# Short-convolution input: c and u of four feature tiles as two jobs of seven block products

## Chip, core and metric

One core of one Trainium2 chip runs the whole kernel in one launch. The metric is the device time of that launch in microseconds (us), lower is better. Differences of a few us in about a thousand are at stake, so every term below is worked out in tenths of a us.

## What is computed

The reference is a two-layer decoder trunk on 512 tokens of width 1024, in float32. Only the start of the first layer is touched by the change:

```python
def short_conv_mixer(h, w_in, conv_w, w_out):
    bcx = h @ w_in                                   # 1024 -> 3 x 1024
    b_gate, c_gate, u = jnp.split(bcx, 3, axis=-1)
    y = b_gate * causal_depthwise_conv3(c_gate * u, conv_w)
    return y @ w_out

h = x
mix = short_conv_mixer(rmsnorm(h, a_pre_norm[l]), a_w_in[l], a_conv_w[l], a_w_out[l])
h = h + rmsnorm(mix, a_post_norm[l])
```

After it come a SwiGLU feed-forward, a sliding-window attention with sinks, and a second feed-forward. They are the same in both kernels.

## The kernel before

**Number format.** Every matrix product is made of three TensorE passes. A factor is split in a high part (`whi`, `xhi`: a copy rounded to fp32r, made by ScalarE) and a low part (`wlo`, `xlo`: the remainder, a subtraction on VectorE), and `mm3` (L203 to L207) adds whi*xlo, whi*xhi and wlo*xhi in PSUM. So a weight tile of 128x1024 costs one ScalarE instruction and one VectorE instruction (L490, L491) before TensorE may use it.

**The convolution stage.** Features lie on the partitions, the 512 tokens along the free dimension. The 1024 features of each of c, u and b are eight tiles, f = 0 to 7. A projection (`project`, L209) is one such tile: eight blocks of the contraction, three passes each, 24 matmuls of 512 columns into one PSUM bank. The norm of x is not applied to x: a row of factors `rows` (one per token, made by `square`, a power on GpSimd, and the matmuls `pr` at L746 and L747) is multiplied into each projection as it is taken out of PSUM (L767, L770, L783). For each feature tile VectorE then runs three tap instructions (`taps`, L774 and L777), GpSimd multiplies c by u (L771) and the taps by b (L784), and `pair_sums` (L602 to L612) makes the sums and splits that the output projection needs. That projection is itself done by seven block products for the first four feature tiles (`P1` to `P7`, function `seven`).

**What sets the order.** The stage stands in a list, `CONV`: "c2" is the projection of c for tile 2, "P1" a block product, "w0" a weight tile that is only split. Tiles 0 and 1 are written out ahead of the list. `in_line` (L495) walks the list. While job j runs on TensorE it emits the split of the weights of job j+3 (`LINE_LEAD = 3`) and the loads that the seven buffers of raw weights (`N_RAW`) allow, and then the late parts of an earlier job (taps, gates, sums), all but one of those that are due in one go. The instructions of each engine run in the order in which they are emitted, and each engine waits on semaphores. Four pairs of whi and wlo exist (`N_W = 4`). GpSimd's queue also issues DMAs that add up weight blocks in DRAM for the later stages (`sum_on`, `issue`, L559). x is loaded transposed (`xt`) for the projections and once in its own layout (`hs`) for the squares and for the residual update.

Of the kernel before, what the change touches and what calls it, by code (L numbers as in the profile page):

```python
# [16 lines left out]
P = 128  # L17
# [20 lines left out]
    "c2 u2 b2 c3 u3 b3 c4 u4 b4 c5 u5 P1 P5 b5 P6 P3 c6 P7 P2 u6 P4 b6 w0 c7 u7 w1 b7 w2 w3"  # L38
)

# [41 lines left out]
def yoco_kernel(  # L82
# [8 lines left out]
    w_in: bass.AP,  # L91
    w_ob: bass.AP,
# [134 lines left out]
    xt = [halves("xt") for _ in range(KT // 2)]  # L227
    xt = [xt[k // 2][k % 2] for k in range(KT)]
# [217 lines left out]
    class Raw:  # L446


        def __init__(self, *srcs):
            self.srcs = srcs  # L450
            self.widths = [s.shape[0] * S if len(s.shape) == 3 else D for s in srcs]
            self.n = sum(self.widths)

        def fetch(self):
            self.tile, c = wraw.tile([P, D], F32, tag="raw", name=name("raw")), 0
            for src, n in zip(self.srcs, self.widths):
# [4 lines left out]
                nc.sync.dma_start(dst, src)  # L461
                c += n

    class Job:
# [10 lines left out]
        def add(self):  # L475
            if self.make:
                raw = self.raws[0].tile
                nc.vector.tensor_tensor(out=raw, in0=raw, in1=self.raws[1].tile, op=ALU.add)  # L478
# [16 lines left out]
    def in_line(jobs, late, paced=True):  # L495
# [9 lines left out]
        def prepare(j):  # L505
# [3 lines left out]
            while n[0] < len(raws) and (n[0] < N_RAW or raws[n[0] - N_RAW].last <= j):  # L509
                raws[n[0]].fetch()  # L510
                n[0] += 1
# [156 lines left out]
    rows = slot("rrow")  # L668
# [6 lines left out]
    sums = small.tile([P, 4], F32, tag="sums", name=name("sums"))  # L675
    squares = wide("squares")

    def square(b):
        nc.scalar.activation(squares, hs[b], AF.Square, scale=1 / 32,
                             accum_out=sums[:, b : b + 1])  # L680

    with tc.manual_schedule(engines=ALL):

        warm = small.tile([P, 1], F32, tag="warm", name=name("warm"))
        nc.scalar.activation(warm, ones[:, 0:1], AF.Copy)
        idle = bank("idle", ps_pt)
        for _ in range(WARM):
            nc.tensor.matmul(idle[:, :P], ones, ones, start=True, stop=True)

        def first_hi(i, c0, c1):  # L690
            nc.scalar.activation(ws[i][0][:, c0:c1], first[i][:, c0:c1], AF.Copy)

        def first_lo(i, c0, c1):
            nc.vector.tensor_tensor(out=ws[i][1][:, c0:c1], in0=first[i][:, c0:c1],
                                    in1=ws[i][0][:, c0:c1].bitcast(F32), op=ALU.subtract)

        def token_hi(k):
            nc.scalar.activation(xs[k][0], xt[k], AF.Copy, scale=g(G_APRE, k))

        def token_lo(k):  # L700
            nc.vector.scalar_tensor_tensor(
                out=xs[k][1], in0=xt[k], scalar=g(G_APRE, k), in1=xs[k][0].bitcast(F32),
                op0=ALU.mult, op1=ALU.subtract,
            )

        FIRST = {0: [(0, 0, P), (0, P, 384)], 1: [(0, 384, 768)], 2: [(0, 768, D), (1, 0, S)],
                 4: [(1, S, D)], 5: [(2, 0, S)], 6: [(2, S, D)]}
        for k in range(KT):
            pieces = FIRST.get(k, [])
            token_hi(k)  # L710
            for p in pieces:
                first_hi(*p)
            for p in pieces:
                first_lo(*p)
            token_lo(k)
            for i in range(3):
                for t in range(3):
                    n = 3 * k + t
                    whi, wlo = (w[:, n % KT * P : (n % KT + 1) * P] for w in ws[n // KT])
                    nc.tensor.matmul(begun[0][t], (whi, wlo, whi)[i], xs[k][i == 2],  # L720
                                     start=k == i == 0, stop=k == KT - 1 and i == 2)
        later += [fetch(w_in[1, t]) for t in range(len(later), 3)]
        for b in range(NB):
            hs[b] = wide("h")
            nc.sync.dma_start(hs[b], x[b])
        nc.sync.dma_start(mask, tables[:, 2 * S :])
        nc.sync.dma_start(snk, sinks.partition_broadcast(P))
        ws = [split_weights(None, raw, True) for raw in later[:2]]
        square(0)
        square(1)  # L730
        ws.append(split_weights(None, later[2], True))
        square(2)
        square(3)
        project(begun[1][0], ws[0], xs)
        v = small.tile([P, 4], F32, tag="v", name=name("v"))
        nc.vector.tensor_scalar(out=v, in0=sums, scalar1=EPS, scalar2=None, op0=ALU.add)
        nc.gpsimd.tensor_tensor(out=cols, in0=v, in1=mhalf, op=ALU.pow)
        project(begun[1][1], ws[1], xs)
        pr = bank("pr", ps_pt)
        dg, dhi, dlo = slot("dg"), slot("dhi", F32R), slot("dlo", F32R)  # L740
        for b in range(NB):
            nc.vector.tensor_scalar(out=dg[:, b * P : (b + 1) * P], in0=ident,
                                    scalar1=cols[:, b : b + 1], scalar2=None, op0=ALU.mult)
        nc.scalar.activation(dhi, dg, AF.Copy)
        nc.vector.tensor_tensor(out=dlo, in0=dg, in1=dhi.bitcast(F32), op=ALU.subtract)
# [1001 lines left out]
```

## Time and profile before

| | us |
|---|---|
| median of 3 runs | 1013.98 (1012.76 to 1014.38) |
| profiled execution, device time | 1012.5 |
| span of its trace | 1010.7 |
| TensorE busy (PE), matmuls | 1002.3 |
| VectorE (DVE) busy | 887.7 |
| ScalarE (ACT) busy | 588.4 |
| GpSimd (POOL) busy | 203.9 |

1.8 us of the profiled execution lie outside the span of the trace. A matmul's record in the trace is longer than its place in the pipeline: a stream of them overlaps, so that the pace of a stream is read from start to start. "pcub" is a projection's PSUM bank, "raw" a weight tile as loaded, "gx", "gy", "gz" the PSUM banks of a feed-forward's block products, "wlo" and "whi" the halves of a split.

### The profile page before, as it was taken

The numbers are of one execution on the slowest core, as the hardware profiler recorded it, in microseconds if no ns is written. First come the engines' busy times: TensorE is split into PE (matmuls) and PEld (weight loads), VectorE is DVE, ScalarE is ACT, GpSimd is POOL, SyncE is SP. The second block draws the span as 40 slices with busy tenths as digits, with TensorE's granted clock in tenths as the row PEclk, the third lists the DMA queues.
The fourth block names the chain that finished last, engine by engine and source line by source line (L and its number), as shares of the span: only waits on it lengthen the run. The fifth ranks groups of instructions, "written<-read, shape, count | busy, mean of one in ns | idle before, by whom it ended". The sixth has DMA issues, their size and how long they took to land.

```text
span 1010.7 us, 16083 instructions
## 1 busy us (share of the span) xinstructions
PE 1002.3 (99%) x5864; PEld 882.4 (87%) x5864; DVE 887.7 (88%) x1525; ACT 588.4 (58%) x1061; POOL 203.9 (20%) x264
## 2 busy tenths in 40 slices
PE   9999999999999999999999999999999999999997
PEld 8888888999889898898898888789998888989986
DVE  5766767899789999999888998888997999999996
ACT  6322444875656465566385788777666564645641
POOL 0443033102101011000022657321211010110001
PEclk9999999999999999999999999999999999999999
DMA  9997789649979789779603889966999577979742
GB/s 357 293 252 241 180 248 334 185 167 268 334 246 288 250 287 311 240 214 343 209 1 120 225 236 245 303 233 176 295 288 330 167 247 235 284 277 266 247 174 84
DMA packets 66575, 244.50 MB, mean 242 GB/s; under 512 B 7872, under 2 KB 8384, under 8 KB 54720
## 3 DMA queue, kind: packets, MB, share of 16 engines
q1 hardware_dynamic: 51328, 145.98, 38.8%
q0 software_dynamic: 14592, 96.48, 37.6%
q10 hardware_dynamic: 576, 1.02, 0.3%
q8 instruction: 46, 0.75, 0.3%
q14 instruction: 33, 0.27, 0.1%
HBM read 237.15 MB, written 102.76 MB: 336 GB/s over the span
## 4 chain that ended last, share of the span: by engine, by line
PE 97%; DVE 2%; ACT 1%; issue 0%; DVEq 0%
PE gx L1093 15%; PE gx L1096 8%; PE pcub L207 4%; PE pcub L205 4%; PE pcub L206 4%; PE px L206 4%; PE px L205 4%; PE px L207 4%; PE pmix L207 3%; PE pmix L205 3%; PE pmix L206 3%; PE gz L1093 3%; PE gy L206 2%; PE gy L205 2%; PE gy L207 2%; PE pz L206 2%
## 5 line engine op out<-in xcount | busy, mean ns | idle before, releaser
L491 DVE TENSOR_TENSOR wlo<-raw,whi 128x1024 fp32r<-128x1024 f32 x225 | 274.6, 1225 | 33.8 <-ACT whi L490 33.7
L490 ACT ACTIVATE whi<-raw 128x1024 fp32r<-128x1024 f32 x225 | 233.7, 1051 | 99.1 <-DVE raw L478 28.7
L1093 PE MATMUL gx<-xt,whi 128*128 128x512 f32 x480 | 120.7, 393 | 0.0
L1093 PEld LDWEIGHTS gx<-xt,whi 128*128 128x128 f32 x480 | 86.2, 189 | 15.7
L559 POOL DMA_DIRECT2D hsum<-in_w_gb_dram x96 | 64.4, 757 | 135.0 <-ACT whi L490 89.6
L559 POOL DMA_DIRECT2D hsum<-hsum x32 | 25.3, 792 | 304.8 <-ACT whi L490 219.7
L1048 DVE TENSOR_TENSOR st<-gx,st 128x256 f32<-128x256 f32 x200 | 77.5, 419 | 2.2 <-ACT st L1071 0.4
L1071 ACT ACTIVATE st<-gx 128x256 f32<-128x256 f32 x120 | 43.5, 380 | 60.9 <-PE gx L1096 57.2
L1096 PEld LDWEIGHTS gx<-xt,wlo 128*128 128x128 f32 x480 | 65.5, 190 | 4.7
L1096 PE MATMUL gx<-xt,wlo 128*128 128x256 f32 x480 | 66.9, 282 | 0.0
L1107 ACT ACTIVATE gr<-gr 128x1024 f32<-128x1024 f32 x20 | 21.2, 1062 | 55.6 <-DVE gr L1048 55.6
L205 PE MATMUL px<-wlo,ahi 128*128 128x512 f32 x120 | 46.7, 389 | 0.0
L206 PE MATMUL px<-whi,ahi 128*128 128x512 f32 x120 | 46.7, 389 | 0.0
L207 PE MATMUL px<-whi,alo 128*128 128x512 f32 x120 | 46.7, 389 | 0.0
L205 PE MATMUL gy<-xlo,whi 128*128 128x256 f32 x160 | 45.3, 283 | 0.0
L206 PE MATMUL gy<-xhi,whi 128*128 128x256 f32 x160 | 45.3, 283 | 0.0
L207 PE MATMUL gy<-xhi,wlo 128*128 128x256 f32 x160 | 45.3, 283 | 0.0
L559 POOL DMA_DIRECT2D hsum<-in_w_dn_dram x48 | 32.6, 794 | 47.3 <-ACT whi L490 47.3
L1093 PE MATMUL gx<-xhl,whi 128*128 128x512 f32 x160 | 39.9, 391 | 0.0
L312 POOL TENSOR_TENSOR ur<-uv,mhalf 128x1 f32<-128x1 f32 x15 | 13.9, 929 | 119.8 <-DVE uv L308 119.8
L660 DVE TENSOR_TENSOR mix<-mix,px 128x512 f32<-128x512 f32 x54 | 34.8, 682 | 2.2 <-PE px L207 2.2
L478 DVE TENSOR_TENSOR raw<-raw,raw 128x1024 f32<-128x1024 f32 x28 | 34.1, 1219 | 0.0
(322 smaller groups left out, 2996.8 us busy)
## 6 DMA issues: line engine op xcount, KB each, us to landing
hsum<-in_w_gb_dram POOLq DMA_DIRECT2D x96, 512.0 KB, 8.0
raw<-hsum SPq DMA_DIRECT2D x88, 512.0 KB, 7.9
raw<-in_w_gb_dram SPq DMA_DIRECT2D x60, 512.0 KB, 7.0
hsum<-in_w_dn_dram POOLq DMA_DIRECT2D x36, 512.0 KB, 8.2
raw<-in_w_dn_dram SPq DMA_DIRECT2D x32, 512.0 KB, 6.2
hsum<-hsum POOLq DMA_DIRECT2D x28, 512.0 KB, 5.7
raw<-in_w_in_dram SPq DMA_DIRECT2D x21, 512.0 KB, 7.4
hsum<-in_w_dn_dram POOLq DMA_DIRECT2D x12, 768.0 KB, 12.1
```

Source lines behind the costliest of these rows:

```text
L205: nc.tensor.matmul(out, whi, xlo, start=start, stop=False, **kw)
L206: nc.tensor.matmul(out, whi, xhi, start=False, stop=False, **kw)
L207: nc.tensor.matmul(out, wlo, xhi, start=False, stop=stop, **kw)
L478: nc.vector.tensor_tensor(out=raw, in0=raw, in1=self.raws[1].tile, op=ALU.add)
L490: self.begun = nc.scalar.activation(hi[:, :n], raw, AF.Copy)
L491: nc.vector.tensor_tensor(out=lo[:, :n], in0=raw, in1=hi[:, :n].bitcast(F32), op=ALU.subtract)
L559: nc.gpsimd.dma_start(dst, src, max_dma_last_dim=4 * 4 * S, **kw))
L660: nc.vector.tensor_tensor(out=m, in0=m, in1=banks[bs][r], op=ALU.subtract if half else ALU.add)
L1048: nc.vector.tensor_tensor(out=out, in0=a, in1=b, op=ALU.add)
L1071: nc.scalar.activation(ste, a, AF.Copy)
L1093: nc.tensor.matmul(banks[c][e], whi[:, kk], factors[p][k][2], start=opened and k == 0, stop=False, **kw)
L1096: nc.tensor.matmul(banks[c][e][:, :256], wlo[:, kk], factors[p][k][0], start=False, stop=k == 3 and p in (4, 5), **kw)
```

## The change

Tiles 0, 1, 6 and 7 keep their projections. For tiles 2 to 5 the order is new: the four projections of b come first (`b2 b3 b4 b5`, `gate_job`), and the eight projections of c and u become two jobs, X for tiles 2 and 3 and Y for tiles 4 and 5, of seven block products each (`cross_jobs`). c and u of a pair of tiles are a two-by-two block product of weights and tokens (the contraction in two halves, the tokens in two halves of 256), and each of the seven products has 24 matmuls of 256 columns. The sums of weight blocks are made on VectorE, four of 128x1024 for each job. The sums of token blocks are made ahead, in the buffers of `xt` (`combine`, `sum_hi`, `sum_lo`), which loses the plain x; x in its own layout is loaded once for the squares, which also overwrite it (`own`), and a second time behind job Y for the residual. The product c*u comes out of PSUM in one step (the last two rows of `take`), so the factor of the norm is squared (`rows2`) and multiplied in once for both. The two matmuls `pr` stand behind the projection b1 rather than ahead of it.

```diff
-    "c2 u2 b2 c3 u3 b3 c4 u4 b4 c5 u5 P1 P5 b5 P6 P3 c6 P7 P2 u6 P4 b6 w0 c7 u7 w1 b7 w2 w3"
+    "b2 b3 b4 b5 X1 X2 X6 X5 X7 X3 X4 Y1 Y2 Y6 Y5 Y7 Y3 Y4 P1 P5 c6 P6 P3 u6 P7 P2 b6 P4 w0 c7 u7 w1 b7 w2 w3"
+CROSS = (2, 6)
...
+    def combine(k):
+        q11, q21, q12, q22 = (quarter(i, hf, k) for hf in range(2) for i in range(2))
+        g0, g1 = g(G_APRE, k), g(G_APRE, k + 4)
+        for out, a, sc, op, b in ((q11, q11, g0, ALU.subtract, q12),
+                                  (q12, q22, g1, ALU.subtract, q12),
+                                  (q22, q22, g1, ALU.add, q11),
+                                  (q21, q21, g1, ALU.subtract, q22)):
+            nc.vector.scalar_tensor_tensor(out=out, in0=a, scalar=sc, in1=b, op0=ALU.mult,
+                                           op1=op)
...
+        def square_rows():
+            nc.vector.tensor_tensor(out=cu, in0=cu, in1=rows2, op=ALU.mult)
...
+    def gate_job(f, pool):
+        def products(job):
+            ps = bank("pcub", pool)
+            project(ps, job.w, xs)
+            brs[f] = slot("bry")
+            nc.vector.tensor_tensor(out=brs[f], in0=ps, in1=rows, op=ALU.mult)
+        return Job([Raw(w_in[f, 2])], products)
+
+    def cross_jobs(f, c):
+        a11, a12, a21, a22 = (Raw(w_cu[f // 2 - 1, b]) for b in range(4))
+        both_of = Raw()
...
+        def plus(out, a, b):
+            nc.vector.tensor_tensor(out=out.tile, in0=a.tile, in1=b.tile, op=ALU.add)
+        def make_two():
+            plus(both_of, a21, a22)
+        def make_three():
+            plus(a21, a21, a11)
+            plus(a11, a11, both_of)
+        def make_four():
+            plus(a12, a12, a11)
+        raws = {1: [a11], 2: [a12, both_of, a21, a22], 6: [a11, a21, both_of], 5: [both_of],
+                7: [a21], 3: [a12, a11], 4: [a22]}
+        make = {2: make_two, 6: make_three, 3: make_four}
...
+        def take(p):
+            x, y, z = (banks.get(c) for c in "XYZ")
+            st, u, gr = kept
+            g0, g1 = (gr.rearrange("p (e h c) -> p e h c", e=2, h=2)[:, :, h] for h in range(2))
+            if p in (1, 6):
+                nc.scalar.activation(st, x, AF.Copy)
+            elif p == 5:
+                nc.scalar.activation(u, z, AF.Copy)
+            elif p == 2:
+                nc.vector.tensor_tensor(out=g0, in0=tiles(y), in1=tiles(st), op=ALU.add)
+            elif p == 3:
+                nc.vector.tensor_tensor(out=g1, in0=tiles(z), in1=tiles(st), op=ALU.add)
+            elif p == 7:
+                nc.vector.tensor_tensor(out=u, in0=x, in1=u, op=ALU.add)
+            else:
+                for gg, m in ((g0, x), (g1, u)):
+                    nc.vector.scalar_tensor_tensor(out=gg, in0=tiles(m), scalar=-1.0, in1=gg,
+                                                   op0=ALU.mult, op1=ALU.mult)
...
+                for e in range(2):
+                    for k in range(4):
+                        kk = slice(e * S + k * P, e * S + (k + 1) * P)
+                        mm3(banks[c][:, e * 256 : (e + 1) * 256], whi[:, kk], wlo[:, kk],
+                            *factors[p][k], ...)
+                take(p)
...
+        def end():
+            steps = [conv(f + e, kept[2], brs.pop(f + e)) for e in range(2)]
+            parts = [lambda: [s[0]() for s in steps], steps[0][1], steps[1][1],
+                     lambda: [s[2](None) for s in steps]]
+            for s in steps:
+                parts += s[3]()
+            return parts
...
     def late():
         parts = []
+        pr = bank("pr", ps_pt)
+        nc.tensor.matmul(pr, ones_r, dlo, start=True, stop=False)
+        nc.tensor.matmul(pr, ones_r, dhi, start=False, stop=True)
+        nc.scalar.activation(rows, pr, AF.Copy)
+        nc.scalar.activation(rows2, pr, AF.Square)
```

What follows of this in each engine's order is shown at three places. On TensorE, behind the projection b1 (its last matmul has wlo_397 before), the projections c2, u2, b2 and so on followed:

```order
L205 MATMUL pcub_245<-xlo_231,whi_395 128x512
L206 MATMUL pcub_245<-xhi_230,whi_395 128x512
L207 MATMUL pcub_245<-xhi_230,wlo_397 128x512
L205 MATMUL pcub_559<-xhl_220,whi_513 128x512
L206 MATMUL pcub_559<-xhl_220,whi_513 128x512
L207 MATMUL pcub_559<-xhl_220,wlo_514 128x512
```

Now b2 to b5 stand there, and behind b5 (pcub_734) comes the product X1, whose matmuls have half the columns:

```order
L209 MATMUL pcub_734<-xhi_230,whi_635 128x512
L210 MATMUL pcub_734<-xhi_230,wlo_636 128x512
L208 MATMUL gx_768<-xhl_220,whi_688 128x256
L209 MATMUL gx_768<-xhl_220,whi_688 128x256
L210 MATMUL gx_768<-xhl_220,wlo_689 128x256
L208 MATMUL gx_768<-xhl_221,whi_688 128x256
```

In all 192 matmuls of 512 columns are gone and 336 of 256 columns have come.

On VectorE, before, the late parts of tiles 2 and 3 (b's gate, then the pair sums of L602 to L612) stand between the low halves of two weight tiles like this; the taps stand further ahead, between other weight tiles:

```order
L783 TENSOR_TENSOR bry_691<-pcub_759,rrow_232 128x512
L602 TENSOR_TENSOR a_218_798<-yy_558,a_218_798 128x256
L605 TENSOR_TENSOR s_796<-yy_558 128x256
L606 SCALAR_TENSOR_TENSOR s_796<-s_796,yy_558 128x256
L605 TENSOR_TENSOR s_797<-yy_558 128x256
L606 SCALAR_TENSOR_TENSOR s_797<-s_796,yy_558 128x256
L612 TENSOR_TENSOR alo_842<-s_796,ahi_841 128x512
L767 TENSOR_TENSOR cru_799<-pcub_802,rrow_232 128x512
L491 TENSOR_TENSOR wlo_872<-raw_588,whi_871 128x1024
```

Now the late parts of both tiles stand in one piece between the low half of Y5's weights (wlo_1030) and that of Y7's (wlo_1086, the last row here). Ahead of these twelve rows stand wlo_1030, the two multiplications by rows2 (`gr`) and the first two taps of tile 2:

```order
L847 SCALAR_TENSOR_TENSOR t_994<-gr_767,gt,t_994 128x510
L844 TENSOR_SCALAR t_996<-gr_767,gt 128x512
L847 SCALAR_TENSOR_TENSOR t_996<-gr_767,gt,t_996 128x511
L847 SCALAR_TENSOR_TENSOR t_996<-gr_767,gt,t_996 128x510
L609 TENSOR_TENSOR a_244_999<-yy_995,a_244_999 128x256
L612 TENSOR_TENSOR s_997<-yy_995 128x256
L613 SCALAR_TENSOR_TENSOR s_997<-s_997,yy_995 128x256
L612 TENSOR_TENSOR s_998<-yy_995 128x256
L613 SCALAR_TENSOR_TENSOR s_998<-s_997,yy_995 128x256
L619 TENSOR_TENSOR alo_1050<-s_997,ahi_1049 128x512
L923 TENSOR_TENSOR gr_1002<-gy_1059,st_1000 128x2x256
L498 TENSOR_TENSOR wlo_1086<-raw_862,whi_1085 128x1024
```

On ScalarE the high half of Y7's weights (whi_1085) stands behind two conversions of the same late parts: `a_244` waits for a GpSimd product (yy_995), `ahi_1049` for a VectorE sum (s_997):

```order
L497 ACTIVATE whi_1029<-raw_861 128x1024
L608 ACTIVATE a_244_999<-yy_995 128x256
L618 ACTIVATE ahi_1049<-s_997 128x512
L497 ACTIVATE whi_1085<-raw_862 128x1024
L618 ACTIVATE ahi_1090<-s_998 128x512
L618 ACTIVATE ahi_1094<-yy_995 128x512
L919 ACTIVATE st_1000<-gx_1003 128x512
L497 ACTIVATE whi_1123<-raw_639 128x1024
```

Before, the same conversions of tiles 2 and 3 stood between whi_827 and whi_912, each about one projection apart.

More of the change, by code (lines that the diff above doesn't have):

```diff
@@ L667, in yoco_kernel @@
           for k in range(KT)]
-    rows = slot("rrow")
+    rows, rows2 = slot("rrow"), slot("rrow")
     cols = small.tile([P, 4], F32, tag="cols", name=name("cols"))
@@ L673, in yoco_kernel @@
              for f in range(2)]
[L675 to L676 removed]
+    sums = small.tile([P, 8], F32, tag="sums", name=name("sums"))
+    own = [[slot("own") for _ in range(2)] for _ in range(NB)]
     def square(b):
[L679 to L745, printed above, removed]
[L746 to L749 removed]
```

244 lines of the change are left out of this document (200 added, 44 removed).

## The prediction

> **What bounds the kernel now.** I read the page's busy times first, then the chain of work that ended last, then the waits of TensorE, and last the windows of the convolution stage.
>
> ```profile
> span 1010.7 us, 16083 instructions
> PE 1002.3 (99%) x5864; PEld 882.4 (87%) x5864; DVE 887.7 (88%) x1525; ACT 588.4 (58%) x1061; POOL 203.9 (20%) x264
> PE 97%; DVE 2%; ACT 1%; issue 0%; DVEq 0%
> PE idle L688 <- DVE ones L149: 1.1, 1, 1.1
> PE pt L1412 <- DVE plo L1429: 0.4, 1, 0.4
> 40.00:50.00 10.00, 10.00 (x46) 8.29 (x45) 7.91 (x14) 2.03 (x4) 5.57 (x7) 1.00 1.04 297
> 90.00:100.00 10.00, 10.00 (x46) 8.29 (x45) 4.68 (x6) 1.58 (x2) 2.01 (x2) 1.00 1.01 340
> ```
>
> TensorE is the chain (97%) and waits 1.5 us in the whole run. In the stage of the change it is busy 10.00 of 10 us (second number of the windows), at a granted clock of 1.00, while VectorE (fourth number) has 2 to 5 us free in ten. So matmul work saved comes off the end one for one, and a wait that TensorE did not have goes on the end one for one. Nothing behind the stage can take it back.
>
> **Part 1, the matmuls.** A projection's 24 matmuls run from the first row to the second; a product's 24 of 256 columns, in the feed-forward, from the third to the fourth.
>
> ```profile
> 149.93 0.39 PE L205 MATMUL pcub<-xhl,whi 128*128 128x512 f32 x1
> 155.37 0.39 PE L205 MATMUL pmix<-wlo,yhi 128*128 128x512 f32 x1
> 206.46 0.28 PE L205 MATMUL gy<-xlo,whi 128*128 128x256 f32 x1
> 209.34 0.63 PE L1093 MATMUL gx<-xt,whi 128*128 128x512 f32 x2
> ```
>
> That is 5.44 us a projection and 2.88 us a product: a matmul of half the columns costs 0.120 us, not half of 0.227. Eight projections go (43.5 us), fourteen products come (40.3 us). The gain is **3.2 us**, if TensorE never waits.
>
> **Part 2, what VectorE must do in the meantime.** Eight projections needed eight weight splits in 43.5 us; fourteen products need fourteen in 40.3 us, plus eight sums of 128x1024. The lead is still three jobs, now 8.6 us instead of 16.3. Prices are starts of neighbouring rows:
>
> ```profile
> 33.13 0.60 ACT L748 ACTIVATE rrow<-pr 128x512 f32<-128x512 f32 x1 [2.35 <-PE pr L747]
> 33.76 0.69 DVE L767 TENSOR_TENSOR cru<-pcub,rrow 128x512 f32<-128x512 f32 x1 [1.64 <-ACT rrow L748]
> 34.37 0.68 DVE L770 TENSOR_TENSOR cru<-pcub,rrow 128x512 f32<-128x512 f32 x1
> 41.94 0.48 DVE L774 TENSOR_SCALAR cut<-cut,gt 128x512 f32<-128x512 f32 x1
> 42.45 1.54 DVE L777 SCALAR_TENSOR_TENSOR cut<-cut,gt 128x511 f32<-128x511 f32 x2
> 43.91 0.69 DVE L783 TENSOR_TENSOR bry<-pcub,rrow 128x512 f32<-128x512 f32 x1
> 47.48 0.41 DVE L605 TENSOR_TENSOR s<-yy 128x256 f32<-128x256 f32 x1
> 49.06 0.69 DVE L612 TENSOR_TENSOR alo<-s,ahi 128x512 fp32r<-128x512 f32 x1
> 73.86 0.41 DVE L602 TENSOR_TENSOR a<-yy,a 128x256 fp32r<-128x256 f32 x1
> 57.59 1.22 DVE L491 TENSOR_TENSOR wlo<-raw,whi 128x1024 fp32r<-128x1024 f32 x1
> 58.72 0.68 DVE L783 TENSOR_TENSOR bry<-pcub,rrow 128x512 f32<-128x512 f32 x1
> 95.07 1.22 DVE L478 TENSOR_TENSOR raw<-raw,raw 128x1024 f32<-128x1024 f32 x1
> 96.20 0.69 DVE L789 TENSOR_TENSOR ylo<-bry,yhi 128x512 fp32r<-128x512 f32 x1
> ```
>
> An operation on 512 columns takes 0.60 us (33.76 to 34.37), three taps 1.97 (41.94 to 43.91), the four pair sums 1.58 (47.48 to 49.06) and the subtraction ahead of them 0.41, a split or a sum of 1024 columns 1.13.
>
> I follow VectorE to the place shown in the change, the low half of Y7's weights (wlo_1086). It can begin its first work of the stage, the taking out of tile 0, only when `rows` is there. That was at 33.76, right behind `pr`; `pr` now stands behind one more projection, so 33.76 + 5.44 = **39.2**. From there to wlo_1086 its queue holds, counted in its order:
>
> - 26 operations on 512 columns (tiles 0 and 1, the token sums of the second half, the four gates, what is taken out of X and of Y2, the two products by rows2, four low halves of pair sums): 15.6 us
> - 13 weight splits and 7 weight sums of 1024: 22.6 us
> - taps of four tiles: 7.9 us; pair sums of two pairs with their subtractions: 4.0 us
>
> That is **50.1 us** with nothing in its way. Two things are. First, GpSimd:
>
> ```profile
> 66.64 1.29 POOL L771 TENSOR_TENSOR cut<-cru 128x512 f32<-128x512 f32 x1 [5.79 <-DVE cru L770]
> 66.67 2.34 DVE L491 TENSOR_TENSOR wlo<-raw,whi 128x1024 fp32r<-128x1024 f32 x1 [0.17 <-ACT whi L490]
> 74.02 1.40 POOL L784 TENSOR_TENSOR yy<-cut,bry 128x512 f32<-128x512 f32 x1 [4.34 <-DVE bry L783]
> 75.45 0.43 DVE L605 TENSOR_TENSOR s<-yy 128x256 f32<-128x256 f32 x1 [1.18 <-POOL yy L784]
> 54.75 1.06 ACT L490 ACTIVATE whi<-raw 128x1024 fp32r<-128x1024 f32 x1 [2.78 <-issue]
> ```
>
> A split beside a GpSimd product takes 2.34 instead of 1.22 us. Three such products of the first two pairs fall beside VectorE's taps or splits (the second c*u, the first gate of each pair): **3.3 us**. Second, waits in VectorE's own queue: the second gate product of a pair starts only behind the last tap, and the pair sums stand behind it (1.18 us in the row; two pairs, 2.0), and a weight that has just been summed must go through ScalarE (1.06 us) before its low half: X3's weights fully, X6's for half of it, and two more behind ScalarE's taking out of X1 and X5, together **2.8 us**. In all 39.2 + 50.1 + 3.3 + 4.8 = 97.4: wlo_1086 is there at about 97.4.
>
> TensorE's side: `pr` began at 32.63 in the row below, so b2 begins 5.44 + 0.46 later, at 38.5; four projections and eleven products (X1 to X4, Y1, Y2, Y6, Y5) are 21.8 + 31.7 us, and two matmuls of Y7 need only its high half: it wants wlo_1086 at **92.2**.
>
> ```profile
> 32.63 0.23 PE pr L746
> ```
>
> So TensorE has waited 5.2 us by then, a little of it ahead of X6 and most at Y7, where the late parts of tiles 2 and 3 stand between two weight splits: some 11 us of VectorE's time, with its wait and its contention, against the 8.6 us of lead. Here the ScalarE order is as bad: whi_1085 stands behind a conversion that waits for the same GpSimd product.
>
> Behind it two smaller waits. Y3's weights are summed, and split behind two low halves, after wlo_1086: 1.13 + 0.60 + 0.60 + 1.13 = 3.5 us against the 2.9 us of Y7: **0.6 us**. P3's weights stand behind the taps of tiles 4 and 5: from Y4's end VectorE has one split in hand and takes out Y4 (1.9), two splits, a sum and ScalarE's part of it (4.5), the products by rows2 and the first taps (3.2); then GpSimd (1.3), three ScalarE operations on 512 columns (1.8, at the 0.60 of the row of `rows`), the high half and the low half (2.2): 14.9 us, while TensorE has P1, P5, c6, P6 (three of 2.72 us and 5.44), 13.6: **1.3 us**.
>
> The sum of the waits is 5.2 + 0.6 + 1.3 = **7.1 us**, against 3.2 gained: **3.9 us slower**.
>
> **Part 3, costed at nothing.** The sixteen token combinations and eight low halves of token sums on VectorE, with their ScalarE operations: the combinations and four of the low halves lie beside c1 and u1, where the 20 to 30 us window has VectorE busy 4.31 of 10 us; the other four are in the count above. Uncovered, the first part would be 6.3 + 2.4 us (16 at the 0.395 of a pair sum, four at 0.60), but `pr` has 5.4 us more time than before. The second loading of x (2 MB) and the halved loads of the first: the queue's loads land in 7.4 us in the median and are wanted some 70 us later. Y's last weight tiles are loaded only when X5's and X7's splits have freed buffers (about 68 and 70 us by the same counting), some 7 us ahead of their sum; late, this costs up to 4 us. GpSimd loses four products and its DMA issues come earlier; both cost TensorE nothing as long as the sums are done before the feed-forward.
>
> ```profile
> 20.00:30.00 10.00, 10.00 (x46) 8.28 (x45) 4.31 (x9) 7.71 (x13) 1.03 (x1) 1.00 1.03 405
> raw<-in_w_in_dram SPq DMA_DIRECT2D x21, 512.0 KB, 7.4
> ```
>
> **Bounds.** No row shows products of this kind fed by VectorE at this lead, so both ends stay. With no contention and no waits VectorE is done at 89.3, ahead of the 92.2, and only the 3.2 us are left. For more than I count speaks a tap instruction beside GpSimd's DMA issues, 1.51 us instead of 0.48:
>
> ```profile
> 36.36 2.23 POOL L559 DMA_DIRECT2D hsum<-in_w_gb_dram  x4
> 37.43 1.51 DVE L774 TENSOR_SCALAR cut<-cut,gt 128x512 f32<-128x512 f32 x1
> ```
>
> With three such groups of issues in its way (3.0 us) and 1.5 us more of waits, the waits sum to 11.6: 8.4 us slower. I take the middle, since each term of it has its own row.
>
> **Rivals.**
>
> - *TensorE never waits.* For it: VectorE had 2 to 5 us free in ten. Against it: its work to Y7 alone, 50.1 us, fills 53 us. It is 3.2 us faster: 1010.8.
> - *The waits only eat the gain.* VectorE's waits overlap GpSimd's contention more than I count; the waits are then 2 to 5 us and the time 1013 to 1016. What decides is whether wlo_1086 comes within 3 us of TensorE's need.
> - *TensorE resumes slowly after its wait at Y7.* The opening shows such a pace: 18 matmuls of 128 columns in 4.20 us (0.23 each), against 16 in 1.67 (0.10, from 175.77 to the next start at 177.44) in full stream.
>
> ```profile
> 1.06 4.20 PE idle L688 x18
> 3.00:5.20 2.20, 2.20 (x12) 2.14 (x11) 0.19 (x1) 1.42 (x4) 0.00 (x0) 1.00 1.01 350
> 175.77 1.91 PE L350 MATMUL xt<-ident,xn 128*128 128x128 f32 x16
> 177.44 0.48 PE L205 MATMUL pmix<-wlo,yhi 128*128 128x512 f32 x1
> ```
>
>   The opening lost 18 * 0.13 = 2.3 us so; with that the time is 1020.2. The granted clock reads 1.00 in the opening's window too (seventh number of the row, behind POOL), and before has no later wait above 0.4 us to look at. The Trainium skill, "TensorE: Matmul & The Clock Gate", Part 1, says that the clock halves after an idle window of about 3.4 us and comes back after a busy one. By that rule the 5 us wait would cost about 1.7 us more, an estimate from that page; here the opening's pace agrees with it, its granted clock does not.
> - *The loads for Y come late.* Up to 4 us more: 1021.9.
> - *The change does not do what it says:* the pace of 0.120 us has a row in the same form, so I give this nothing.
>
> **How the numbers follow.** The profiled execution took 1012.5 us, 1.5 below the median of the runs shown. Its own time plus 3.9 is 1016.4; against the median it is 1013.98 + 3.9 = **1017.9**, and all times here are against the median. Forecast (1016 to 1021): 0.60. Waits that only eat the gain: 0.16. No waits: 0.09. Slow resumption: 0.10. Late loads: 0.05. The range of 1013 to 1022 leaves out the third and a few of the highest. About 0.2% (2 us) is what a measurement of this kernel can tell from no change: faster by more 0.10, within 0.15, slower by more 0.75.
>
> **What would show it.** Right: TensorE's waits list names wlo or whi of the weight splits (L498, L497) with 5 to 9 us in sum between 60 and 130 us, one wait of 4 us or more at about 93; b2 to b5 at 5.44 us and products at 2.88 us elsewhere; VectorE over 9 of 10 us from 60 to 100. Wrong: TensorE at 10.00 of 10 in those windows (first rival), products of Y7 above 2.88 us (third), VectorE waiting for DMA at the sum of Y's blocks (fourth). The forecast falls if VectorE reaches wlo_1086 before about 93.

## The result, and the profile after

The changed kernel takes 1028.57 us (1028.29 to 1029.04), the kernel before 1013.66 us in the same runs: a ratio of 1.0148, with a 95% interval of 1.013 to 1.0166. It is 14.9 us slower. The forecast was 3.9 us slower, and its range ended at 1022. Each time here and below is the median of a kernel's executions, and one execution of `h_behind` (a run below), of 1657 us at a granted clock of 0.56, is left out.

First the page of the profile after (busy times and the chain of work that ended last), then the list of what TensorE waited for in the whole span: waiter, releaser, us in total, times, longest.

```profile
span 1027.2 us, 16455 instructions
PE 1005.9 (98%) x6008; PEld 890.5 (87%) x6008; DVE 920.3 (90%) x1569; ACT 603.8 (59%) x1094; POOL 198.6 (19%) x260
PE 89%; DVE 6%; ACT 2%; DMA 1%; issue 1%; POOL 1%; DVEq 0%; SPq 0%; ACTq 0%; POOLq 0%
PE gx L208 <- ACT st L919: 7.0, 2, 5.8
PE pmix L208 <- DVE wlo L198: 2.2, 1, 2.2
PE pmix L208 <- ACT yhi L859: 1.6, 1, 1.6
PE pz L208 <- DVE wlo L498: 1.3, 1, 1.3
PE gy L210 <- DVE wlo L498: 0.5, 1, 0.5
PE gx L210 <- DVE wlo L498: 0.3, 1, 0.3
```

Of the chain, TensorE's share has gone from 97% to 89% and VectorE's from 2% to 6%. The list sums to 12.9 us of waits that were not there before. Four groups matter: product 6 of X (1.2 of the 7.0), Y7 (5.8), P3 (1.3), and the output projection `pmix` (2.2 and 1.6).

Y7, on TensorE, then on VectorE, then on ScalarE (start, us, instruction, idle time before it and its releaser):

```profile
95.49 0.28 PE L210 MATMUL gz<-xf,wlo 128*128 128x256 f32 x1
101.58 0.58 PE L208 MATMUL gx<-xf,whi 128*128 128x256 f32 x1 [5.81 <-ACT st L919]
101.96 0.41 PE L209 MATMUL gx<-xf,whi 128*128 128x256 f32 x1
102.17 0.41 PE L210 MATMUL gx<-xf,wlo 128*128 128x256 f32 x1
...
88.75 1.23 DVE L498 TENSOR_TENSOR wlo<-raw,whi 128x1024 fp32r<-128x1024 f32 x1 [0.69 <-ACT whi L497]
89.89 1.29 DVE L841 TENSOR_TENSOR gr<-gr,rrow 128x512 f32<-128x512 f32 x2
93.58 2.45 DVE L847 SCALAR_TENSOR_TENSOR t<-gr,gt,t 128x511 f32<-128x511 f32 x2
97.51 0.43 DVE L612 TENSOR_TENSOR s<-yy 128x256 f32<-128x256 f32 x1 [1.15 <-POOL yy L855]
99.70 0.68 DVE L923 TENSOR_TENSOR gr<-gy,st 128x512 f32<-128x512 f32 x1
100.30 1.21 DVE L498 TENSOR_TENSOR wlo<-raw,whi 128x1024 fp32r<-128x1024 f32 x1
...
98.43 0.63 ACT L618 ACTIVATE ahi<-s 128x512 fp32r<-128x512 f32 x1 [3.28 <-DVE s L613]
100.95 0.57 ACT L919 ACTIVATE st<-gx 128x512 f32<-128x512 f32 x1
```

The split for Y5 starts at 88.75, that for Y7 at 100.30. Between them stand the late parts of tiles 2 and 3 in one piece, 9.8 us from 89.89 to 99.70, with the contention (2.45 us where two taps take 1.54) and the wait for GpSimd that the prediction had in it. The releaser of Y7's first matmul is not this split, though, but ScalarE's copy of the bank that Y6 has filled (`st`, L919): it stands on ScalarE behind the high half of Y7's weights and three conversions of the same late parts, one of which waited 3.28 us for VectorE's sums. Copy and split end together (100.95 + 0.57 = 101.52, 100.30 + 1.21 = 101.51), so that either alone would have held Y7 about as long; no run moves the parts in one queue and not in the other. The product behind the wait is slow: 0.21 us from start to start (101.96 to 102.17) in place of 0.12. The windows show why (time; then busy us of PE, PEld, DVE, ACT, POOL; then the granted clock, the share of the DMA engines, GB/s):

```profile
98.00:100.00 2.00, 0.00 (x0) 0.00 (x0) 1.98 (x5) 1.57 (x3) 2.00 (x5) 0.86 0.79 66
104.00:106.00 2.00, 2.00 (x11) 2.00 (x11) 1.80 (x2) 2.00 (x3) 0.00 (x0) 0.50 0.94 318
106.00:108.00 2.00, 2.00 (x18) 2.00 (x17) 1.62 (x3) 0.12 (x1) 0.00 (x0) 0.94 1.03 425
```

The granted clock falls to 0.50 while TensorE stands still, and comes back only near 106. Y7 takes 5.03 us (101.58 to the next product at 106.61) in place of 2.88.

The end of the stage, which the prediction did not reach: first ScalarE, then the sync queue that loads the feed-forward's first weights (`w_gu`), then TensorE in the output projection.

```profile
154.44 0.63 ACT L859 ACTIVATE yhi<-bry 128x512 fp32r<-128x512 f32 x1 [3.33 <-POOL bry L855]
154.98 1.14 ACT L192 ACTIVATE whi<-raw 128x512 fp32r<-128x512 f32 x2
...
167.78 1.06 ACT L435 ACTIVATE whi<-raw 128x1024 fp32r<-128x1024 f32 x1 [5.98 <-DMA raw<-in_w_gu_dram]
168.75 0.61 ACT L192 ACTIVATE whi<-raw 128x512 fp32r<-128x512 f32 x1
173.33 0.63 ACT L859 ACTIVATE yhi<-bry 128x512 fp32r<-128x512 f32 x1 [3.96 <-DVE bry L855]
...
144.91 12.45 SPq L172 DMA_DIRECT2D raw<-in_w_gu_dram  x4
...
171.42 0.50 PE L208 MATMUL pmix<-wlo,yhi 128*128 128x512 f32 x1 [2.17 <-DVE wlo L198]
174.01 0.50 PE L208 MATMUL pmix<-wlo,yhi 128*128 128x512 f32 x1 [1.62 <-ACT yhi L859]
176.18 0.63 PE L210 MATMUL pmix<-whi,ylo 128*128 128x512 f32 x1
176.61 0.63 PE L208 MATMUL pmix<-wlo,yhi 128*128 128x512 f32 x1
```

Read it from the bottom. `pmix` waits for the last low half of `w_out` (L198) and the last high half of y (L859). The high halves of both stand on ScalarE behind the split of the fourth `w_gu` tile (L435 at 167.78), and ScalarE stood there 5.98 us for its load. That load was late: the four issues reach from 144.91 over 12.45 us, since each needs a free raw buffer. Of the queue's waits for them, two (4.0 and 4.2 us) are put down to splits of `w_out` (L198), the later of which stands behind a y that goes over GpSimd (3.33 us of waiting at 154.44), and two (0.7 and 6.0 us) to splits of the stage's last weights (L498). Behind the two waits the projection runs at 0.43 us a matmul (176.18 to 176.61) in place of 0.23, until about 178.

Where the 16.5 us between the two spans went, each from the starts of TensorE's instructions in the two traces (the medians lie 14.9 us apart: the profiled execution is above the median for the changed kernel and below it for the one before):

| | us |
|---|---|
| opening, up to the matmuls `pr` (39.02; before's 32.47 and a projection of 5.44 give 37.91) | +1.1 |
| fourteen products for eight projections | -3.2 |
| X2 and X6: waits of 1.9 and slow restarts | +2.7 |
| Y7: from the wait of 5.81 | +6.0 |
| Y7: half clock | +2.1 |
| P3: wait of 1.3 | +1.6 |
| output projection: waits of 3.8, then slow matmuls | +6.2 |

The sum is 16.5. The first is no part of the change: the other kernels below open in the same way and reach `pr` between 38.04 and 38.89. It goes with the clock: the first step to full clock that the trace records is at 7.27 us here and at 5.13 us before, and of the kernels below the two with the latest such step (7.20 in `h_behind`, 7.11 in `one_ring_five`) reach `pr` last (38.89 and 38.80).

### The profile page after: what moved, and what is told of

Its sections match the earlier page's. It is cut to its first block, busy times and chain, and to the rows that moved or that the text cites. A ratio compares the mean times of both kernels' runs of the same rounds, so it can differ in the third digit from the quotient of the medians.

```text
span 1027.2 us, 16455 instructions
## 1 busy us (share of the span) xinstructions
PE 1005.9 (98%) x6008; PEld 890.5 (87%) x6008; DVE 920.3 (90%) x1569; ACT 603.8 (59%) x1094; POOL 198.6 (19%) x260
## 4 chain that ended last, share of the span: by engine, by line
PE 89%; DVE 6%; ACT 2%; DMA 1%; issue 1%; POOL 1%; DVEq 0%; SPq 0%; ACTq 0%; POOLq 0%
PE gx L1283 14%; PE gx L1286 7%; PE px L208 3%; PE px L209 3%; PE px L210 3%; PE pmix L210 3%; PE pmix L208 3%; PE pmix L209 3%; PE gz L1283 3%; PE gy L209 2%; PE gy L208 2%; PE gy L210 2%; PE pcub L774 2%; PE pz L208 2%; PE pz L209 2%; PE pz L210 2%
## 5 line engine op out<-in xcount | busy, mean ns | idle before, releaser
L498 DVE TENSOR_TENSOR wlo<-raw,whi 128x1024 fp32r<-128x1024 f32 (+1 forms) x231 | 279.4, 1214 | 28.2 <-ACT whi L497 28.0
L497 ACT ACTIVATE whi<-raw 128x1024 fp32r<-128x1024 f32 (+1 forms) x231 | 239.7, 1050 | 89.9 <-DVE raw L485 34.4
L210 PE MATMUL gy<-xhi,wlo 128*128 128x256 f32 x176 | 49.9, 284 | 0.5 <-DVE wlo L498 0.5
L208 PE MATMUL gy<-xlo,whi 128*128 128x256 f32 x176 | 49.8, 283 | 0.0
L209 PE MATMUL gy<-xhi,whi 128*128 128x256 f32 x176 | 49.8, 283 | 0.0
L210 PEld LDWEIGHTS gy<-xhi,wlo 128*128 128x128 f32 x176 | 33.8, 192 | 0.7 <-DVE wlo L498 0.7
```

The lines of the kernel that those rows point to most:

```text
L208: nc.tensor.matmul(out, whi, xlo, start=start, stop=False, **kw)
L209: nc.tensor.matmul(out, whi, xhi, start=False, stop=False, **kw)
L210: nc.tensor.matmul(out, wlo, xhi, start=False, stop=stop, **kw)
L497: self.begun = nc.scalar.activation(hi[:, :n], raw, AF.Copy)
L498: nc.vector.tensor_tensor(out=lo[:, :n], in0=raw, in1=hi[:, :n].bitcast(F32), op=ALU.subtract)
```

## The experiments

All ratios are against the kernel before, run on the same chip in the same session, with their 95% intervals.

| run | us | ratio |
|---|---|---|
| late_one | 1016.97 | 1.0036 [1.0024, 1.0047] |
| tail | 1023.49 | 1.0101 [1.0076, 1.0127] |
| h_behind | 1027.59 | 1.0144 [1.0127, 1.0161] |
| ring | 1029.27 | 1.0157 [1.014, 1.0174] |
| warm | 1029.25 | 1.0158 [1.0143, 1.0173] |
| late_from_p | 1021.40 | 1.0085 [1.0068, 1.0102] |
| one_ring | 1015.04 | 1.0022 [1.0013, 1.0032] |
| one_gate | 1018.02 | 1.0051 [1.0036, 1.0066] |
| late_to_p | 1028.09 | 1.0148 [1.0134, 1.0161] |
| one_ring_early | 1011.46 | 0.9986 [0.9977, 0.9995] |
| one_ring_five | 1017.78 | 1.0037 [1.0024, 1.0049] |
| ring_early | 1028.10 | 1.015 [1.0133, 1.0167] |

**Is it the place of VectorE's late parts, or the amount of its work?** `late_one`:

```diff
-            for _ in range(1 if paced else max(len(late) - 1, 1)):
+            for _ in range(1):
```

> One deferred part of a convolution step is put into the queue per job in place of all but one; nothing else is changed. Theory 'place': Y7 waits because six deferred parts (9.8 us of VectorE, from 89.89 to 99.70) stand in one piece between the splits for Y5 and Y7. Then the 5.8 us wait before Y7 and the half-clock stretch behind it (2.15 us) go, some 2 to 4 us come back as waits near P1, and the time is 1022 to 1025 us. Theory 'amount': VectorE simply has more work up to there than TensorE has products, so that the wait only moves to P1 to P6; it stays at 6 us or more in all, and the time is 1026 to 1029 us. The waits of the output projection (3.8 us) stay by both.

1016.97 us: 11.6 us of the 14.9 are gone, more than 'place' expected, because the waits at the end of the stage went too, which both theories had staying. TensorE's waits in this run, and the row of VectorE ahead of what is left of them:

```profile
PE gx L208 <- DVE st L927: 1.9, 1, 1.9
PE gx L208 <- ACT st L919: 1.2, 1, 1.2
PE gy L210 <- DVE wlo L498: 0.4, 1, 0.4
PE pmix L208 <- ACT yhi L859: 0.2, 1, 0.2
...
81.16 1.22 DVE L895 TENSOR_TENSOR raw<-raw,raw 128x1024 f32<-128x1024 f32 x1 [4.35 <-issue]
```

Y7, P3 and `pmix` no longer wait; the second job has four smaller waits, 3.7 us in all. The same work fits: it was the place.

**What holds the output projection?** Three small edits, each on the changed kernel alone. `tail` moves P4 one job forward:

```diff
-    "b2 b3 b4 b5 X1 X2 X6 X5 X7 X3 X4 Y1 Y2 Y6 Y5 Y7 Y3 Y4 P1 P5 c6 P6 P3 u6 P7 P2 b6 P4 w0 c7 u7 w1 b7 w2 w3"
+    "b2 b3 b4 b5 X1 X2 X6 X5 X7 X3 X4 Y1 Y2 Y6 Y5 Y7 Y3 Y4 P1 P5 c6 P6 P3 u6 P7 P2 P4 b6 w0 c7 u7 w1 b7 w2 w3"
```

> The last of the seven products, P4, stands ahead of the projection b6 in place of behind it; nothing else is changed. Theory 'lead': the output projection waits 2.17 and 1.62 us and then runs at half clock because ScalarE stands at P4's eviction until P4 has ended, and only three projections follow P4 in the changed kernel where four followed it before, so that the splits and the loads behind that eviction come 5.4 us closer to their use. Then those waits and the half-clock stretch behind them (6.2 us in all) shrink to 0 to 2 us, P4 may wait up to 1.5 us for its own weights, and the time is 1022 to 1025 us. Theories 'second load' (the 2 MB of x loaded again fill the transfers) and 'ring' (the loads fall behind because two of the seven raw buffers hold sums, and the sync queue stands still from 77 to 90 us): the last load of the w_gu weights still lands about 2 us after it is wanted, and the time stays at 1027 to 1029 us.

1023.49 us, 5.1 less, as 'lead' expected for the time. But the four executions lie between 1021.58 and 1026.46, and the profiled one is that of 1026.46. In it the mechanism is only half that: ScalarE still waits 5.1 and 4.2 us for two `w_gu` loads, and one wait of the output projection is left.

```profile
PE pmix L208 <- ACT yhi L859: 2.6, 1, 2.6
```

`h_behind` issues the second load of x behind the first weights of the feed-forward:

```diff
-                for b in range(NB):
-                    hs[b] = wide("h")
-                    nc.sync.dma_start(hs[b], x[b])
...
     ahead = Ahead(first_weights(0))
+    for b in range(NB):
+        hs[b] = wide("h")
+        nc.sync.dma_start(hs[b], x[b])
```

> The second load of x (four loads of 512 KB) is issued behind the w_gu and w_gb loads in place of ahead of the w_out loads; nothing else is changed. Theory 'second load': the last w_gu load lands some 5 us sooner, the waits of the output projection go (6.2 us with the half clock behind them), and the time is 1022 to 1025 us, unless x itself then comes late for the first update at about 181 us. Theories 'lead' and 'ring': the waits stay, 1027 to 1030 us.

1027.59 us, and `pmix` waits 2.5 and 1.6 us as ever. The 2 MB loaded twice cost nothing that this run can tell from the changed kernel (ratios 1.0144 and 1.0148).

`ring` gives the kept sum its own buffer:

```diff
+        both_of.tile = wide("both")
...
-                if raw not in raws:
+                if raw not in raws and raw.srcs:
```

> The sum of two weight blocks that each job of seven products keeps is put into a buffer of its own, so that all seven raw buffers take loads; nothing else is changed. Theory 'ring': the sync queue no longer stands still from 77 to 90 us, the loads behind it come earlier by up to 10 us, the w_gu loads too, and the waits of the output projection shrink: 1022 to 1025 us. Theory 'lead': the queue's stop goes, but the w_gu loads still wait for buffers that the w_out splits free at 156 to 157 us, and the time stays within 1 us of 1028.6.

1029.27 us. The two buffers that held sums are not what holds the end: the queue's stop from 78 to 90 us goes, but the `w_gu` loads are issued as before, from 144.10 over 12.43 us.

So the cause had to lie in the order. `late_from_p` changes the late parts from P1 on alone (job 18), and `late_to_p` the half ahead of it (the same line with `j < 18`):

```diff
-            for _ in range(1 if paced else max(len(late) - 1, 1)):
+            for _ in range(1 if paced or j >= 18 else max(len(late) - 1, 1)):
```

> One deferred part per job from P1 on, and all but one per job ahead of it as in the changed kernel, so that Y7's wait stays. Theory 'place' for the end of the stage: there too it is the parts in one piece that do it, since the third part of c6 to b6 with its way over GpSimd stands on ScalarE ahead of the split of the w_out weights, which frees the buffers for the w_gu loads; then the 6.2 us at the output projection go but for 0 to 1.5 us, Y7's 8.1 us stay, and the time is 1022 to 1024.5 us. Theory 'follows from Y7': the end's waits come from the loads that Y7's wait has pushed together, and the time stays at 1027 to 1029 us.

> The complement: one deferred part per job ahead of P1, and all but one per job from P1 on, as in the changed kernel. Theory 'two places': Y7's piece and the piece at the third parts of c6 to b6 act by themselves. Then Y7's wait and the half clock go (8.1 us, less some 4 us of shorter waits in the second job that come back), but P3's and the output projection's waits stay at 5 us or more: 1022 to 1025 us. Theory 'one place': the end's waits follow only from Y7's, and the time is that of one part per job in the whole line, 1016.5 to 1018 us.

`late_from_p` takes 1021.40 us. Y7's wait is untouched, and the end and P3 are free but for 0.4 us, which accounts for the 7.2 us that are gained. ScalarE shows the mechanism: the two splits of `w_out` (L192) now stand ahead of the y over GpSimd (L859), and the fourth `w_gu` split waits for TensorE and no longer for its load.

```profile
PE gx L208 <- ACT st L919: 7.0, 2, 5.8
PE pmix L208 <- ACT yhi L859: 0.4, 1, 0.4
...
148.13 1.14 ACT L192 ACTIVATE whi<-raw 128x512 fp32r<-128x512 f32 x2
151.87 0.63 ACT L859 ACTIVATE yhi<-bry 128x512 fp32r<-128x512 f32 x1 [2.60 <-POOL bry L855]
162.78 1.06 ACT L435 ACTIVATE whi<-raw 128x1024 fp32r<-128x1024 f32 x1 [3.86 <-PE pcub L209]
```

`late_to_p` takes 1028.09 us, against the 1022 to 1025 of 'two places' and the 1016.5 to 1018 of 'one place'; both missed. Y7's wait is gone, but nothing is gained: waits in the second job come back, `pmix` waits 2.3 and 1.6 us, the parts that were not done there fall in one piece ahead of P3, and the clock falls to about half three times (the third at 172 us, in the output projection). So the two places do not add: undoing the pieces up to Y7 alone gives 0.5 us, those behind it alone 7.2, both together 11.6.

```profile
PE pz L208 <- DVE wlo L498: 3.4, 1, 3.4
PE gx L208 <- DVE st L927: 1.9, 1, 1.9
104.00:106.00 2.00, 2.00 (x11) 2.00 (x11) 1.94 (x4) 0.58 (x1) 0.58 (x1) 0.50 1.05 417
126.00:128.00 2.00, 2.00 (x7) 1.53 (x7) 1.71 (x2) 0.81 (x1) 0.00 (x0) 0.61 0.37 90
```

**Is the slow Y7 the clock?** `warm` fills the wait with matmuls into a bank that nobody reads:

```diff
+                if f == 4 and p == 7:
+                    busy = bank("busy", ps_pt)
+                    for _ in range(24):
+                        nc.tensor.matmul(busy, ones_r, xs[0][0], start=True, stop=True)
```

> 24 matmuls of 512 columns (5.4 us), into a bank that nobody reads, stand in TensorE's queue just ahead of Y7's product; the deferred parts stand in one piece as in the changed kernel. They fill the 5.8 us in which TensorE waits for Y7's split. Theory 'clock': the 2.15 us that Y7's product takes too long are the price of the idle stretch, so the granted clock stays at 1.00 behind the wait, Y7 takes 2.9 us, and the time falls by about 2 us to 1026.0 to 1027.0. Theory 'neighbours': the slow pace comes from what else runs then (splits, transfers), the clock still falls to about 0.5, and the time stays within 0.5 us of 1028.6.

In the profiled execution the wait is 0.23 us and Y7's product runs at its pace (0.12 from start to start, 2.97 us to the next product), beside the same splits and loads:

```profile
100.75 0.39 PE L208 MATMUL gx<-xf,whi 128*128 128x256 f32 x1 [0.23 <-ACT st L919]
100.97 0.28 PE L209 MATMUL gx<-xf,whi 128*128 128x256 f32 x1
101.09 0.28 PE L210 MATMUL gx<-xf,wlo 128*128 128x256 f32 x1
PE pz L208 <- DVE wlo L498: 2.2, 1, 2.2
```

So the 2.1 us are the price of standing still. The granted clock of this execution reads 0.95 where the others read 1.00, at the same pace of matmuls, and does not fall at Y7; it falls to 0.50 at 169.6 us, in the output projection. The time did not fall, though: the median is 1029.25. Counted from `pr`, P1 starts 1.6 us sooner than in the changed kernel (71.70 us behind `pr`, against 73.34), and P3's wait takes 0.9 of it back; what the other executions did, which have no trace, is open. A gain at Y7 meets the next thing that VectorE has not done.

**What is left with one part per job?** `one_ring` is `late_one` and `ring` together. `one_gate` is `late_one` with b5 moved:

```diff
-    "b2 b3 b4 b5 X1 X2 X6 X5 X7 X3 X4 Y1 Y2 Y6 Y5 Y7 Y3 Y4 P1 P5 c6 P6 P3 u6 P7 P2 b6 P4 w0 c7 u7 w1 b7 w2 w3"
+    "b2 b3 b4 X1 X2 X6 X5 X7 X3 X4 Y1 b5 Y2 Y6 Y5 Y7 Y3 Y4 P1 P5 c6 P6 P3 u6 P7 P2 b6 P4 w0 c7 u7 w1 b7 w2 w3"
```

> One deferred part per job in the whole line, and the kept sum of two blocks in a buffer of its own, so that all seven raw buffers take loads. With one part per job alone VectorE stands still from 76.7 to 81.2 us for the second job's blocks (transfer engines idle from 60 to 68 us). Theory 'ring': that stop goes, VectorE is 3 to 4 us ahead in the second job, the waits of 0.4, 1.2, 0.3 and 1.9 us there shrink to 1 us in all, and the time is 1012.5 to 1015 us. Theory 'chain': those waits come from the chain sum, split, product of each job and not from the loads, and the time stays at 1016.5 to 1017.5 us.

> One deferred part per job in the whole line, and the gate projection b5 moved from ahead of X1 to between Y1 and Y2. TensorE then has 5.4 us of other work in front of Y2 to Y4 and 5.4 us less in front of X1. Theory 'amount': the waits of the second job (3.7 us and some 1.3 us of slow pace) go and the first job, which waited for nothing, pays 0 to 2 us: 1012.5 to 1015 us. Theory 'chain': the first job now waits as the second did, and the time is 1016 to 1018 us.

`one_ring` takes 1015.04 us, 1.9 less than `late_one` and just outside the range of 'ring'. VectorE's stop shrinks only from 4.35 to 3.04 us, and is now put down to the load itself:

```profile
79.77 1.23 DVE L896 TENSOR_TENSOR both<-raw,raw 128x1024 f32<-128x1024 f32 x1 [3.04 <-DMA raw<-in_w_cu_dram]
```

Both theories were partly right: by the code the four blocks of X hold their buffers until X7, X3 and X4, so Y's still come late. `one_gate` takes 1018.02 us, the upper end of 'chain': the waits get smaller and more (0.4 at X4, and 0.8, 0.4, 0.7, 1.0, 1.2 in Y). But the first job does not wait as the second did, as 'chain' said; it has the 0.4 alone.

`one_ring_early` shortens the chain and frees a buffer sooner, on top of `one_ring`:

```diff
         def make_three():
-            plus(a21, a21, a11)
             plus(a11, a11, both_of)
         def make_four():
+            nc.vector.tensor_tensor(out=a21.tile, in0=a11.tile, in1=a22.tile, op=ALU.subtract)
             plus(a12, a12, a11)
...
-        raws = {1: [a11], 2: [a12, both_of, a21, a22], 6: [a11, a21, both_of], 5: [both_of],
-                7: [a21], 3: [a12, a11], 4: [a22]}
-        make = {2: make_two, 6: make_three, 3: make_four}
+        raws = {1: [a11], 2: [a12, both_of, a21, a22], 6: [a11, both_of], 5: [both_of, a11, a12, a21, a22],
+                7: [a21], 3: [a12], 4: [a22]}
+        make = {2: make_two, 6: make_three, 5: make_four}
```

> One deferred part per job, the kept sum in a buffer of its own, and in both jobs the sum a11+a21+a22 is made first, with a21+a11 as its difference to a22 and a12's sum made right behind it, so that product 6 waits for one addition in place of two and the buffer of a11 comes free two products sooner. Theory 'chain and loads': VectorE's stop of 3.0 us at 76.7 us shrinks to 0 to 1.5 us, and of the waits of 0.5, 0.3 and 1.9 us in the second job at most 1 us is left: 1012.0 to 1014.0 us, level with before or just under it. Theory 'VectorE full': the 1.9 us before the second job's last product are VectorE's backlog, and stay: 1014.5 to 1015.5 us.

1011.46 us, ratio 0.9986 [0.9977, 0.9995]: **faster than both kernels**, by 1.3 us than before (0.5 to 2.3 by the interval). All of TensorE's waits in the run, apart from the 1.1 us at its start, and two windows of the products:

```profile
PE pt L1603 <- DVE plo L1620: 0.4, 1, 0.4
PE pmix L208 <- ACT yhi L859: 0.2, 1, 0.2
60.00:80.00 20.00, 20.00 (x167) 19.92 (x166) 19.46 (x25) 9.57 (x13) 6.39 (x7) 1.00 0.68 150
80.00:100.00 20.00, 20.00 (x169) 20.00 (x168) 19.82 (x22) 7.90 (x10) 9.11 (x10) 1.00 1.01 344
```

TensorE is busy 20.00 of 20 us and VectorE 19.46 and 19.82. So 'VectorE full' is wrong as the cause of the waits, but barely: in these 40 us it has 0.7 us to spare. Of the 3.2 us that the matmuls save, about half reach the end: without a wait in the list, P1, P5 and c6 take 0.5 us longer than before, the last three projections 0.3 and the output projection 0.7. Why is open.

`one_ring_five` goes one step further, product 5 ahead of product 6:

```diff
-    "b2 b3 b4 b5 X1 X2 X6 X5 X7 X3 X4 Y1 Y2 Y6 Y5 Y7 Y3 Y4 P1 P5 c6 P6 P3 u6 P7 P2 b6 P4 w0 c7 u7 w1 b7 w2 w3"
+    "b2 b3 b4 b5 X1 X2 X5 X6 X7 X3 X4 Y1 Y2 Y5 Y6 Y7 Y3 Y4 P1 P5 c6 P6 P3 u6 P7 P2 b6 P4 w0 c7 u7 w1 b7 w2 w3"
...
-        make = {2: make_two, 6: make_three, 5: make_four}
+        make = {2: make_two, 6: make_three, 7: make_four}
```

> As the run with the early sum, and product 5, which needs only the kept sum, stands ahead of product 6 in both jobs, so that the sum for 6 has 2.9 us more. Theory 'chain and loads': product 6 waits for nothing any more, and the time is that of the early sum less 0 to 0.8 us: 1011.5 to 1013.5 us. Theory 'VectorE full': the wait only moves behind it, to product 7 or 4, and the time is within 0.5 us of the early sum's.

1017.78 us, 6.3 slower than without it; both theories missed. Products 6 and 7 add to the same PSUM bank, and ScalarE must copy it between them. Product 5 stood between and hid that copy. Now X7 waits 2.07 us for it, since two conversions of the late parts stand ahead of it on ScalarE (73.11 to 74.17), and runs at half clock behind the wait (74.80 to 79.26; 0.50 from 76 to 78 us). The five executions lie between 1015.37 and 1017.98, and the profiled one is that of 1017.98. `st` is the copy:

```profile
PE gx L208 <- ACT st L920: 2.8, 2, 2.1
```

Last, `ring_early` has all of `one_ring_early` except the one part per job:

> The kept sum in a buffer of its own and the sum for product 6 made first, as in the fastest run, but the deferred parts in pieces of all but one, as in the changed kernel. Theory 'place': the piece of 9.8 us still stands ahead of Y7's split, and the piece at the end of the stage ahead of the w_out splits; the 1.2 us of waits before product 6 of the first job go, but Y7's wait (some 5 us with 2 us of half clock) and the output projection's 6 us stay: 1024 to 1028 us. Theory 'sums and loads': it is the order of the sums and the loads that makes the fastest run, and the pieces cost little beside them: 1012 to 1018 us.

1028.10 us, the changed kernel's time, with Y7 at 6.0 us of wait and `pmix` at 3.0 and 1.6. The better sums and loads are worth 0.5 us at most while the late parts come in pieces, and 5.5 us (1016.97 to 1011.46) once they do not: 1.9 for the loads and 3.6 for the sums.

## Why the prediction was wrong

Its sign held, its size did not: 3.9 us forecast, 14.9 measured. By its own steps:

- **Part 1 held.** In `one_ring_early` the fourteen products take 40.31 us (60.33 to 100.64), as worked out (40.3).
- **Part 2 up to Y7 held in mechanism, and was too small.** The list of waits has Y7 with 5.8 us at 95.6, where 4 us or more at about 93 were forecast, and the piece between the splits is 9.8 us long, where some 11 were forecast. `late_one` and `ring_early` show that this place, and not VectorE's total, is the cause. The sign that was named did not come: the list puts the wait down to ScalarE's copy `st` and not to a split. The sum had no term for that copy; that it ended together with wlo_1086 is luck. VectorE was at 8.0 to 9.3 of 10 us from 60 to 100, and not over 9, since it waited too. The 97.4 counts the split wlo_1086 itself as its thirteenth, so it stands against 101.4, the end of the split: 4.0 us too small, 1.1 of it because the first work on VectorE began at 40.31 and not at 39.2. TensorE lost 8.7 us up to Y7's start where 5.2 were forecast, 2.7 of it at X2 and X6, which the prediction had as "a little" ahead of X6.
- **P3 held** (1.3 forecast, 1.3 measured), while Y3's 0.6 did not come: Y7 ran so slowly that Y3's weights were in time.
- **The step that failed is "Behind it two smaller waits".** The sum ended at P3. The same rule that put the piece ahead of Y7 also puts the last tiles' parts ahead of the splits of `w_out`, and through buffers and loads this reaches ScalarE's queue and the output projection: 6.2 us that no term held. `late_from_p` removes all but 0.4 us of their waits by the order alone, and `h_behind` and `ring` show that neither the second load of x nor the two raw buffers that hold sums are the cause. I had followed the engines' queues only as far as the new jobs went.
- **The slow resumption was a rival at 0.10 and belonged in the sum.** A forecast that holds a wait of 5 us has to price it. It was put at 2.3 us by the opening's pace and measured at 2.1 at Y7, and there is more of it in the output projection's 6.2 (3.8 are waits). That the opening's granted clock read 1.00 was no evidence against it: the trace of before records its first step to full clock only at 5.13 us, and the windows show 1.00 for the time ahead of it, of which it records nothing. The Trainium skill, "TensorE: Matmul & The Clock Gate", Part 1, which gave 1.7 us by its rule, names the right mechanism: the granted clock reads 0.50 behind the wait, and `warm` removes it.
- **Part 3 held where it was tested.** The second load of x cost nothing. The late loads for Y, a rival at 0.05, are real but stood behind the larger wait: VectorE's stop shows only once the pieces are gone (4.35 us in `late_one`, 3.04 in `one_ring`).

The range failed with the sum: its upper bound of 11.6 us of waits left out both the end of the stage and the clock.

## What to carry to other kernels

When an engine that had two to five tenths of its time free becomes nearly full, the order in the queues can be worth more than its total: here the same work cost 14.9 us in pieces and 3.9 us when it was dealt out one part per job (1016.97 against 1013.11). Follow such a rule through every place at which it acts, up to the next stage's first loads, and not only where the diff stands. To a TensorE wait of some 4 us or more in a forecast, add the half-clock stretch behind it; a wait of about 2 us may bring one or not, as the next section shows. And do not add up what single repairs should give: here one of two repairs was worth 0.5 us without the other.

## What the runs showed of the hardware

Whether a wait of about 2 us halves the clock is not decided by its length alone. Behind 1.91 us (`late_one`) the next product took 2.94 us and the clock stayed at 1.00; behind 1.92 us at the same place (`late_to_p`) it took 4.39 us, at 0.50. The windows from 104 to 106 us are the one of `late_one` here and the first one shown for `late_to_p` above:

```profile
104.00:106.00 2.00, 2.00 (x16) 1.91 (x16) 1.97 (x4) 0.71 (x1) 0.45 (x1) 1.00 1.04 416
```

It depends on where the wait falls. Between its first and its last step, each trace changes the granted clock only at whole multiples of 3.413 us: in the changed kernel it is full for 27 of these windows, half for two (99.43 to 106.26 us), full for 20 and half for one (174.53 to 177.94). With the windows counted from those steps, the clock fell to half behind every window between 55 and 180 us in which TensorE, at full clock, waited 1.92 us or more in sum (sixteen cases in nine of the thirteen traces of the new order), and behind none with 1.90 or less. The 1.92 us of `late_to_p` lie in one window (100.23 to 103.65). The 1.91 us of `late_one` are cut into 0.28 and 1.63, and a wait of 2.20 us at P3 in `warm` into 1.55 and 0.65; neither was followed by half clock. By this count a wait of twice 1.92 us would be followed by half clock wherever it falls. Each half clock lasted one window or two.
